# Prompt attention of a two-layer hybrid model: from split fp32r matmuls of one head group to plain fp32 matmuls of two head groups on array halves

## The chip, the core and the metric

The kernel runs on one core of a Trainium2 chip. The metric is the device time of one execution in microseconds (us); the number quoted for a kernel is the median of several executions. TensorE (PE in the profile) multiplies, VectorE (DVE), ScalarE (ACT) and GpSimd (POOL) do elementwise work, SyncE (SP) here only issues DMAs. ScalarE and GpSimd issue DMAs too; each engine takes its instructions in order, DMA issues among them.

## The reference, cut to what matters

Two layers are computed for a prompt of 512 tokens and for a decode batch of 8 sequences with 4 new tokens each. Layer 0 is a gated delta-rule mixer, layer 1 a sparse attention (NSA), each followed by a convolutional feed-forward part. The attention of layer 1 has 16 query heads in 4 groups; a group has one key head and one value head of width 64. Per head, three results are mixed with three learned gates:

```
o_c = attention over compressed blocks of 64 tokens   (raw queries)
o_s = attention over the blocks that o_c selects      (rotated queries)
o_w = attention over a sliding window                 (rotated queries)
out = (g0 * o_c + g1 * o_s + g2 * o_w) @ w_out
```

For the prompt, with 512 tokens and so 8 blocks, `o_s` and `o_w` are both causal attentions over all 512 tokens, with different keys and values. For the decode batch the compressed and the selected keys come from a paged cache in HBM.

## The kernel before, in words

`nsa` runs the attention of layer 1. It has two stages in which several generators ("streams") are merged by `attend`: each stream yields the cost of the piece that it has just emitted, and the stream whose sum of costs is the smallest share of its total goes next. The totals are written by hand: `(22.0, 14.0, 22.0)` for the first stage, `(116.0, 112.0)` for the second. The framework then orders instructions once more with its own model of their times, so an engine's final order can differ from the order in which the code emits them; page loads of the cache are excepted, they stay in the order written. The order of each engine is fixed before the kernel runs.

First stage: `nsa_compress` multiplies cached pages with compression weights (L1523, 8 groups of 32 steps, 64x64 tiles of the array, one accumulator bank of `ps` for each row half). Its page loads (L1467) are issued alternately by SP and POOL, with a page number read from memory ahead of each. Beside it run `cmp_sample` (selection for the decode batch) and `cmp_prompt` (`o_c` of the prompt). `cmp_prompt` reads the eight tiles of raw queries back from HBM through a tile `qx` of two buffers (L1570, SP's queue) and multiplies each (L1571) into one bank.

Second stage: `nsa_sample`, the decode batch, turns cached keys (L1924, copies L1927 and L1929), multiplies scores (L1936), exponentiates and multiplies values (L1995), 16 steps of a sequence and a branch. Beside it `nsa_prompt` works through 32 units (g, n, br): head group g, query head n of it, and branch br (0 for `o_s`, 1 for `o_w`). A unit has three steps, of which one loop pass emits `scores` for unit s, `turn` for unit s-1 and `values` for unit s-2:

- `scores`: every fp32 number is split into a high and a low part of type fp32r. The tile `qs` holds the high part of the query in one half of the 128 rows and the low part in the other; `kh` and `kl` are the parts of the key, in both halves. Each 128 queries take two matmuls (L1780, L1781) of 128x128 weights and 256, 256, 384 or 512 columns. L1783 adds the causal mask and takes the maximum, L1785 exponentiates, L1790 (POOL) scales by gate over sum.
- `turn`: ten transposes (L1805) into three banks, and each bank is split by a cast (L1808, ACT) and a subtraction (L1809, DVE).
- `values`: eight matmuls (L1825) with the high and low part of the values side by side as weights; L1829 and L1830 add the two halves. The result of an even group goes to HBM (`oad`) and is read back when the odd group is done, `o_c` is added (L1837) and the sum goes to `od`.

PSUM has eight banks: two for `po` and `pos`, three for `ps` (nsa_compress and nsa_sample), three for `pp` (nsa_prompt). After the second stage `nsa_out` reads `od` and multiplies with the output weights.

Of the kernel before, what the change touches and what calls it, by code (L numbers as in the profile page):

```python
# [167 lines left out]
class K:  # L168
# [35 lines left out]
    def pool(self, ctx, name, bufs=1, **kw):  # L204
        return ctx.enter_context(self.tc.tile_pool(name=name, bufs=bufs, reuse_waits="tile", **kw))
# [1008 lines left out]
    def nsa(self, nctx, dctx, sctx):  # L1214
# [16 lines left out]
        N['oad'] = [dr.tile([64, 512], F32, name="oad%d" % n) for n in range(4)]  # L1231
        N['kvcd'] = dr.tile([128, 4, 512], F32, name="kvcd")
        with ExitStack() as xctx:
# [44 lines left out]
        for w in self.attend([second(), self.nsa_prompt(kp, ap)], (116.0, 112.0)):  # L1278
            pass
# [269 lines left out]
    def cmp_prompt(self, sp, cP, place):  # L1549
# [182 lines left out]
    def nsa_prompt(self, kp, ap):  # L1732
        nc, N, tc = self.nc, self.N, self.tc
        units = [(g, n, br) for g in range(4) for n in range(4) for br in range(2)]
        KV, QS, PO, EE, PT = {}, {}, {}, {}, {}
        off = (0, 128, 384, 768)

        def keys(g):
            gp, a = divmod(g, 2)
            own, oth = slice(a * 64, a * 64 + 64), slice(64 - a * 64, 128 - a * 64)  # L1740
            for br in range(2):
                kd = kp.tile([128, 512], F32, name="kd", bufs=2)
                for h in (own, oth):
                    nc.scalar.dma_start(kd[h], N['krd'][br][gp][own])
                kh = kp.tile([128, 512], F32R, name="kh%d" % br, bufs=2)
                kl = kp.tile([128, 512], F32R, name="kl%d" % br, bufs=2)
                nc.scalar.copy(kh, kd)
                nc.vector.tensor_tensor(kl, kd, kh.bitcast(F32), op=OP.subtract)
                vs = kp.tile([128, 4, 64], F32, name="vd")
                nc.scalar.dma_start(vs, N['vnd'][br][:, :, g * 64:(g + 1) * 64])  # L1750
                vv = kp.tile([128, 4, 2, 64], F32R, name="v%d" % br, bufs=2)
                nc.scalar.copy(vv[:, :, a, :], vs)
                nc.gpsimd.tensor_tensor(vv[:, :, 1 - a, :], vs, vv[:, :, a, :].bitcast(F32), op=OP.subtract)
                KV[g, br] = kh, kl, vv

        def scores(u):
            g, n, br = u
            gp, a = divmod(g, 2)
            own, oth = slice(a * 64, a * 64 + 64), slice(64 - a * 64, 128 - a * 64)
            if br == 0:  # L1760
                qd = ap.tile([128, 512], F32, name="qd", bufs=1)
                for h in (own, oth):
                    nc.scalar.dma_start(qd[h], N['qrotd'][gp * 4 + n][own])
                qs = ap.tile([128, 512], F32R, name="qs")
                nc.scalar.copy(qs, qd)
                nc.vector.tensor_tensor(qs[oth], qd[oth], qs[oth].bitcast(F32), op=OP.subtract)
                QS[g, n] = qs
            qs = QS[g, n]
            kh, kl, vv = KV[g, br]
            e = ap.tile([128, 1280], F32, name="e")  # L1770
            mn = ap.tile([128, 4], F32, name="mn")
            sm = ap.tile([128, 4], F32, name="sm")
            p2 = None
            for qt in range(4):
                w = 128 * (qt + 1)
                wm = max(w, 256)
                if qt != 1:
                    p2 = self.pp.tile([128, 512], F32, name="pp")
                p = p2[:, 256:512] if qt == 1 else p2[:, :wm]
                nc.tensor.matmul(p, qs[:, qt * 128:(qt + 1) * 128], kh[:, :wm], start=True, stop=False)  # L1780
                nc.tensor.matmul(p, qs[:, qt * 128:(qt + 1) * 128], kl[:, :wm], start=False, stop=True)  # L1781
                ee = e[:, off[qt]:off[qt] + w]
                nc.vector.tensor_tensor_reduce(out=ee, in0=p[:, :w], in1=self.n('tri')[:, 512 - w:], scale=-0.125, scalar=3e38,  # L1783
                                               op0=OP.add, op1=OP.min, accum_out=mn[:, qt:qt + 1])
                nc.scalar.activation(ee, ee, AF.Exp, scale=-1.0, bias=mn[:, qt:qt + 1], accum_out=sm[:, qt:qt + 1])  # L1785
            nc.vector.reciprocal(sm, sm)
            nc.vector.tensor_tensor(sm, sm, N['gtok'][:, :, (g * 4 + n) * 3 + 1 + br], op=OP.mult)  # L1787
            for qt in range(4):
                ee = e[:, off[qt]:off[qt] + 128 * (qt + 1)]
                nc.gpsimd.tensor_scalar(ee, ee, sm[:, qt:qt + 1], 1.0, op0=OP.mult, op1=OP.mult)  # L1790
            EE[u] = e

        poff = (0, 512, 1024, 896)

        def turn(u):
            e = EE.pop(u)
            ph = ap.tile([128, 1280], F32R, name="pth")
            pl = ap.tile([128, 1280], F32R, name="ptl")
            for kts in ((0,), (1, 3), (2,)):
                p = self.pp.tile([128, 512], F32, name="pp")  # L1800
                at = 0
                for kt in kts:
                    for qt in range(kt, 4):
                        c = off[qt] + kt * 128
                        nc.tensor.transpose(p[:, at:at + 128], e[:, c:c + 128], self.ident)  # L1805
                        at += 128
                s = slice(poff[kts[0]], poff[kts[0]] + at)
                nc.scalar.copy(ph[:, s], p[:, :at])  # L1808
                nc.vector.tensor_tensor(pl[:, s], p[:, :at], ph[:, s].bitcast(F32), op=OP.subtract)  # L1809
            PT[u] = ph, pl  # L1810

        def values(u):
            g, n, br = u
            gp, a = divmod(g, 2)
            own, oth = slice(a * 64, a * 64 + 64), slice(64 - a * 64, 128 - a * 64)
            if br == 0:
                PO[g, n] = self.po.tile([128, 512], F32, name="po")
            po = PO[g, n]
            ph, pl = PT.pop(u)
            vv = KV[g, br][2]  # L1820
            for kt in range(4):
                w = 512 - kt * 128
                vw = vv[:, kt].rearrange("p r e -> p (r e)")
                for part in (ph, pl):
                    nc.tensor.matmul(po[:, kt * 128:], vw, part[:, poff[kt]:poff[kt] + w], start=br == 0 and kt == 0 and part is ph,  # L1825
                                     stop=br == 1 and kt == 3 and part is pl)
            if br:
                t = ap.tile([128, 512], F32, name="ot", bufs=1)
                nc.scalar.copy(t[own], po[oth])  # L1829
                nc.vector.tensor_tensor(t[own], po[own], t[own], op=OP.add)  # L1830
                if a == 0:
                    nc.scalar.dma_start(N['oad'][n], t[own])
                else:
                    oc = ap.tile([128, 512], F32, name="oc", bufs=1)
                    nc.scalar.dma_start(t[oth], N['oad'][n])
                    nc.scalar.dma_start(oc, N['ocd'][gp * 4 + n])
                    nc.gpsimd.tensor_tensor(t, t, oc, op=OP.add)  # L1837
                    nc.scalar.dma_start(N['od'][gp * 4 + n], t)

        nu = len(units)  # L1840
        for s in range(nu + 2):
            if s < nu:
                if s == 0:
                    with self.after((self.cmp_done, self.cmp_out)):
                        keys(0)
                if s % 8 == 4 and s < 28:
                    keys(s // 8 + 1)
                with self.after((self.cmp_done, self.cmp_out) if s == 0 else ()):
                    scores(units[s])
                yield 1.2  # L1850
            if 0 <= s - 1 < nu:
                turn(units[s - 1])
                yield 1.1
            if 0 <= s - 2:
                values(units[s - 2])
                yield 1.2
# [270 lines left out]
```

## Time and profile before

| | us |
|---|---|
| median of 3 executions | 2018.57 (2018.2 to 2020.0) |
| the profiled execution | 2023.65 |
| its span, first to last instruction | 2022.0 |
| PE busy in the span | 1913.4 (95%) |
| DVE, ACT, POOL busy | 1138.1, 793.0, 602.6 |

Matmuls are pipelined, so a matmul's duration contains a tail that lies beside the next ones; what a matmul costs the engine is read from the distance of two starts. A plain fp32 matmul appears as two MATMUL instructions in the trace, a transpose and an fp32r matmul as one.

### The profile page before, as it was taken

How to read it: one execution, taken by the hardware profiler on the slowest of the kernel's cores; microseconds unless marked ns; L12 is line 12 of the kernel's file. 1: busy time of each engine (PE TensorE's matmuls, PEld its weight loads, DVE VectorE, ACT ScalarE, POOL GpSimd, SP SyncE). 2: the span in 40 equal slices, each digit the busy share in tenths (PEclk: the TensorE clock that was granted, in tenths of full speed). 3: DMA queues.
4: the chain of work that ended last, by engine and by line, in shares of the span. 5: the costliest groups of instructions: out<-in, count | busy, mean ns of one | idle time of the engine just before them, and what ended most of it. 6: DMA issues, size and time to landing. Idle time of an engine off the chain costs nothing.

```text
span 2022.0 us, 42933 instructions
## 1 busy us (share of the span) xinstructions
PE 1913.4 (95%) x16796; PEld 1756.5 (87%) x16796; DVE 1138.1 (56%) x2215; ACT 793.0 (39%) x1517; POOL 602.6 (30%) x1164
## 2 busy tenths in 40 slices
PE   7999999989999999989989697999997999999997
PEld 7999878879999999989978374676776999999997
DVE  6675586665755655553330024676665476564654
ACT  5543335443433333342210003665754443342335
POOL 2332445112423322301334211233332243241321
PEclk9999989989999999999999787999998999999999
DMA  5222012142222232265578637687576222223221
GB/s 166 87 89 87 11 45 62 42 143 91 80 90 87 84 97 83 76 188 159 170 218 246 190 118 238 193 251 216 171 220 133 91 85 85 84 86 103 77 83 59
DMA packets 225647, 247.07 MB, mean 122 GB/s; under 512 B 29862, under 2 KB 181334, under 8 KB 225188
## 3 DMA queue, kind: packets, MB, share of 16 engines
q1 hardware_dynamic: 196564, 200.09, 32.7%
q10 hardware_dynamic: 19824, 24.72, 4.2%
q0 software_dynamic: 9056, 19.51, 3.3%
q8 instruction: 132, 2.16, 0.4%
q14 instruction: 71, 0.58, 0.1%
HBM read 211.38 MB, written 32.86 MB: 121 GB/s over the span
## 4 chain that ended last, share of the span: by engine, by line
PE 85%; DMA 6%; DVE 4%; ACT 2%; issue 1%; SPq 1%; POOL 0%; ACTq 0%; DVEq 0%; POOLq 0%
PE pdn L424 59%; PE ps L1523 6%; PE po L1825 2%; DMA kv<-in_cache_sel 1%; PE ps L1936 1%; PE pp L1805 1%; PE ps L1924 1%; PE pos L1995 1%; PE ps L847 1%; PE pp L1780 1%; PE ps L857 1%; DMA od<-od 1%; PE pq L1037 1%; PE pp L1781 1%; PE pq L1001 1%
## 5 line engine op out<-in xcount | busy, mean ns | idle before, releaser
L424 PE MATMUL pdn<-hh,whi 128*128 128x272 f32 (+1 forms) x2272 | 477.3, 291 | 3.1 <-ACT hh L323 2.3
L424 PE MATMUL pdn<-hh,wlo 128*128 128x272 f32 (+1 forms) x2272 | 472.1, 289 | 0.0
L424 PE MATMUL pdn<-hl,whi 128*128 128x272 f32 (+1 forms) x2272 | 470.1, 288 | 0.0
L397 ACT CAST whi<-wraw 128x1024 fp32r<-128x1024 f32 (+3 forms) x222 | 214.2, 966 | 454.1 <-PE pdn L424 393.4
L424 PEld LDWEIGHTS pdn<-hh,whi 128*128 128x128 f32 (+1 forms) x2272 | 357.4, 188 | 6.0 <-ACT hh L323 2.7
L424 PEld LDWEIGHTS pdn<-hl,whi 128*128 128x128 f32 (+1 forms) x2272 | 356.7, 188 | 0.7
L424 PEld LDWEIGHTS pdn<-hh,wlo 128*128 128x128 f32 (+1 forms) x2272 | 354.6, 188 | 1.1 <-issue 0.4
L398 DVE TENSOR_TENSOR wlo<-wraw,whi 128x1024 fp32r<-128x1024 f32 (+3 forms) x222 | 250.7, 1130 | 34.7 <-ACT whi L397 27.6
L1133 DVE SCALAR_TENSOR_TENSOR facc<-fext,par,facc 128x592 f32<-128x592 f32 x176 | 146.2, 831 | 19.5 <-ACT facc L1131 16.7
L453 DVE TENSOR_TENSOR xT<-pdn,xT 128x544 f32<-128x544 f32 x80 | 57.7, 724 | 163.9 <-PE pdn L424 163.9
L1126 POOL COPY fext<-fext 128x32 f32<-128x32 f32 x88 | 31.1, 353 | 393.1 <-DVE fext L1123 392.6
L424 PE MATMUL pdn<-gh,whi 128*128 128x272 f32 x704 | 146.3, 289 | 0.2
L424 PE MATMUL pdn<-gh,wlo 128*128 128x272 f32 x704 | 145.2, 288 | 0.3 <-DVE wlo L398 0.3
L424 PE MATMUL pdn<-gl,whi 128*128 128x272 f32 x704 | 144.9, 288 | 0.0
L1523 PE MATMUL ps<-x,wc 64*64 64x128 f32 (+1 forms) x2048 | 135.9, 401 | 7.9 <-DVE cT L1535 5.6
L1523 PEld LDWEIGHTS ps<-x,wc 64*64 64x64 f32 x2048 | 106.6, 155 | 37.1 <-issue 8.4
L1123 DVE TENSOR_TENSOR fext<-pdn,rstd 128x544 f32<-128x544 f32 x88 | 63.6, 725 | 114.0 <-PE pdn L424 113.3
L424 PEld LDWEIGHTS pdn<-gl,whi 128*128 128x128 f32 x704 | 110.0, 188 | 0.3 <-DVE gl L1147 0.2
L424 PEld LDWEIGHTS pdn<-gh,wlo 128*128 128x128 f32 x704 | 109.6, 188 | 0.8 <-DVE wlo L398 0.8
L424 PEld LDWEIGHTS pdn<-gh,whi 128*128 128x128 f32 x704 | 109.4, 188 | 0.8 <-ACT whi L397 0.7
L1790 POOL TENSOR_SCALAR e<-e,sm 128x128 f32<-128x128 f32 (+3 forms) x128 | 66.5, 540 | 110.1 <-DVE sm L1787 38.2
L1131 ACT ACTIVATE facc<-fext,par 128x592 f32<-128x592 f32 x88 | 77.6, 883 | 41.5 <-POOL fext L1126 41.4
(543 smaller groups left out, 3271.1 us busy)
## 6 DMA issues: line engine op xcount, KB each, us to landing
wraw<-in_ffn_w_up SPq DMA_DIRECT2D x40, 1024.0 KB
kv<-in_cache_sel SPq DMA_DIRECT2D x128, 256.0 KB
x<-in_cache_cmp SPq DMA_DIRECT2D x128, 128.0 KB
wraw<-in_gdn_w_in SPq DMA_DIRECT2D x15, 1024.0 KB
wraw<-in_ffn_w_down SPq DMA_DIRECT2D x16, 768.0 KB
x<-in_cache_cmp POOLq DMA_DIRECT2D x96, 128.0 KB, 3.4
wraw<-in_ffn_w_down SPq DMA_DIRECT2D x16, 640.0 KB
kv<-in_state_win SPq DMA_DIRECT2D x16, 512.0 KB
```

The source lines that it names most:

```text
L397: nc.scalar.copy(h, raw)
L398: nc.vector.tensor_tensor(l, raw, h.bitcast(F32), op=OP.subtract)
L424: nc.tensor.matmul(p[:mw, j, :TH], w[:, k, :mw], (x[k] if type(x) is list else x[:, k, :])[:, j * TH:(j + 1) * TH], start=k == 0 and n == ...
L453: self.nc.vector.tensor_tensor(self.two(self.xT[:, m, :]), p, self.two(self.xT[:, m, :]), op=OP.add)
L847: nc.tensor.matmul(p[:, s], B['na'][h][:, s], Y[h][:, s], start=True, stop=True)
L1123: nc.vector.tensor_tensor(self.two(ext[:, 2:2 + T]), p, self.two(rstd), op=OP.mult)
L1126: nc.gpsimd.tensor_copy(se[:, :, 2:6], ext[:, 514:546].rearrange("p (b j) -> p b j", j=4))
L1131: nc.scalar.activation(acc, ext[:, 0:592], AF.Identity, scale=ws[0], bias=self.pcol(f'ffn_b{i}', ft))
L1133: nc.vector.scalar_tensor_tensor(acc, ext[:, j:592 + j], ws[j], acc, op0=OP.mult, op1=OP.add)
L1523: nc.tensor.matmul(p[par][half(f), :n], W[c][half(par), d, :], x[half(par), :n, d], start=k == 0, stop=k == 31)
L1790: nc.gpsimd.tensor_scalar(ee, ee, sm[:, qt:qt + 1], 1.0, op0=OP.mult, op1=OP.mult)
L1825: nc.tensor.matmul(po[:, kt * 128:], vw, part[:, poff[kt]:poff[kt] + w], start=br == 0 and kt == 0 and part is ph, stop=br == 1 and kt == ...
```

## The change

- The prompt's units become 16: (gp, n, br), a pair gp of head groups. Queries, keys and probabilities stay fp32; no part is split.
- `scores`: the two groups of a pair lie in the two halves of the 128 rows. Two matmuls, one for each half of the rows, write to two banks; `pp` has four banks, `ps` two.
- `values`: two matmuls, one for each half of the columns, write to the two halves of one bank; `o_c` is added straight from PSUM. `oad` is gone.
- `turn` copies the transposes once instead of splitting them.
- Keys and values are loaded once, without copies in the other half.
- The raw queries of `cmp_prompt` are loaded from ScalarE's queue.
- The totals and costs for `attend` are rewritten, and `nsa_prompt` yields in smaller pieces.

```
-        N['oad'] = [dr.tile([64, 512], F32, name="oad%d" % n) for n in range(4)]
...
-            self.psum(pctx, 0, 3)
-            self.pp = pool(pctx, "pp", 3, space=PSUM)
+            self.psum(pctx, 0, 2)
+            self.pp = pool(pctx, "pp", 4, space=PSUM)
...
-            for w in self.attend([groups, self.cmp_sample(sp, cT, rest), self.cmp_prompt(sp, cP, x2)], (22.0, 14.0, 22.0)):
+            for w in self.attend([groups, self.cmp_sample(sp, cT, rest), self.cmp_prompt(sp, cP, x2)], (28.0, 14.0, 22.0)):
...
-        for w in self.attend([second(), self.nsa_prompt(kp, ap)], (116.0, 112.0)):
+        for w in self.attend([second(), self.nsa_prompt(kp, ap)], (116.0, 104.0)):
...
-            nc.sync.dma_start(qx, N['qrawd'][j])
+            nc.scalar.dma_start(qx, N['qrawd'][j])
...
+        units = [(gp, n, br) for gp in range(2) for n in range(4) for br in range(2)]
+        half = lambda h: slice(h * 64, h * 64 + 64)
+        def keys(br):
+            for gp in range(2):
+                K[gp, br] = kp.tile([128, 512], F32, name="k%d%d" % (gp, br))
+                nc.scalar.dma_start(K[gp, br], N['krd'][br][gp])
+            V[br] = kp.tile([128, 4, 256], F32, name="v%d" % br)
+            nc.scalar.dma_start(V[br], N['vnd'][br])
...
         def scores(u):
...
+            es = [ap.tile([128, 1280], F32, name="e", bufs=4) for a in range(2)]
...
+            for qts in ((0, 2), (3,), (1,)):
+                p2 = [self.pp.tile([128, 512], F32, name="pp") for a in range(2)]
+                at = 0
+                for qt in qts:
+                    w = 128 * (qt + 1)
+                    ps = [p[:, at:at + w] for p in p2]
+                    at += w
+                    for a in range(2):
+                        nc.tensor.matmul(ps[a], q[half(a), qt * 128:(qt + 1) * 128], k[half(a), :w], start=True, stop=True)
+                    for a in range(2):
...
+                yield 1.72 * at / 1024
...
         def turn(u):
...
+                    if i == 1:
+                        nc.scalar.copy(t[:, s], p[:, :at])
+                    else:
+                        nc.vector.tensor_copy(t[:, s], p[:, :at])
+                PT[u].append(t)
+                yield 1.1
 
         def values(u):
...
             for kt in range(4):
                 w = 512 - kt * 128
+                for a in range(2):
+                    g = 2 * gp + a
+                    nc.tensor.matmul(po[half(a), kt * 128:], V[br][:, kt, g * 64:(g + 1) * 64], ts[a][:, poff[kt]:poff[kt] + w],
+                                     start=br == 0 and kt == 0, stop=br == 1 and kt == 3)
             if br:
+                oc = ap.tile([128, 512], F32, name="oc", bufs=1)
+                nc.scalar.dma_start(oc, N['ocd'][gp * 4 + n])
                 t = ap.tile([128, 512], F32, name="ot", bufs=1)
+                nc.vector.tensor_tensor(t, PO.pop((gp, n)), oc, op=OP.add)
+                nc.scalar.dma_start(N['od'][gp * 4 + n], t)
...
             if 0 <= s - 2:
                 values(units[s - 2])
-                yield 1.2
+                yield 2.15
```

## Rows read from the trace of the kernel before

**Rows 1.** The page: busy shares, 40 slices, and the chain that ended last.
```profile
PE 1913.4 (95%) x16796; PEld 1756.5 (87%) x16796; DVE 1138.1 (56%) x2215; ACT 793.0 (39%) x1517; POOL 602.6 (30%) x1164
...
PE   7999999989999999989989697999997999999997
...
PE 85%; DMA 6%; DVE 4%; ACT 2%; issue 1%; SPq 1%; POOL 0%; ACTq 0%; DVEq 0%; POOLq 0%
```

**Rows 2.** Busy time by stretch: busy us of engines (x instructions), granted clock, DMA share, GB/s.
```profile
1120.00:1165.00 45.00, 26.90 (x239) 14.84 (x234) 4.81 (x14) 1.55 (x4) 11.88 (x23) 0.75 0.59 180
1165.00:1222.00 57.00, 57.00 (x821) 43.53 (x819) 13.45 (x41) 5.96 (x14) 9.68 (x18) 0.91 0.36 111
1222.00:1262.00 40.00, 29.19 (x133) 16.22 (x129) 19.05 (x57) 14.72 (x35) 5.30 (x9) 0.74 0.91 272
1262.00:1540.00 278.00, 263.62 (x3097) 196.32 (x3096) 186.89 (x627) 180.19 (x491) 96.85 (x176) 0.98 0.65 196
```

**Rows 3.** Timeline of 1105 to 1146 us: start, us, engine, line, [idle before].
```profile
1123.42 1.98 PE L1571 MATMUL po<-qx,lb 128*128 128x512 f32 x4
...
1124.46 17.58 SPq L1467 DMA_DIRECT2D x<-in_cache_cmp  x16
...
1131.64 0.42 ACT L1673 ACTIVATE ss<-ss 64x256 f32<-64x256 f32 x1 [19.70 <-DVE ss L1671]
...
1142.15 0.85 SPq L1570 DMA_DIRECT2D qx<-qrawd  x2
...
1145.85 1.22 PE L1571 MATMUL po<-qx,lb 128*128 128x512 f32 x1 [18.10 <-DMA qx<-qrawd]
```

**Rows 4.** Timeline of PE, 1341 to 1345 us: one unit of the prompt.
```profile
1341.27 0.50 PE L1825 MATMUL po<-pth,v 128*128 128x512 f32 x1
...
1344.22 0.28 PE L1781 MATMUL pp<-kl,qs 128*128 128x256 f32 x1
1344.43 0.23 PE L2006 MATMUL ps<-cf,e 64*32 64x64 f32 x1
```

**Rows 5.** Timeline of PE, 1437 to 1441 us: column halves, then transposes.
```profile
1437.48 1.94 PE L1936 MATMUL ps<-kt,qf 128*64 128x512 f32 x8
1439.35 1.31 PE L1805 MATMUL pp<-cf,e 128*128 128x128 f32 x10
1440.50 0.71 PE L1924 MATMUL ps<-cf,kv 128*128 128x128 f32 x5
```

**Rows 6.** Timeline of PE, 287 to 290 us: one row half, one matmul after another.
```profile
287.77 1.93 PE L1037 MATMUL pq<-wg,dkd 64*128 64x512 f32 x4
289.63 0.60 PE L847 MATMUL ps<-Y,na 128*128 128x128 f32 x3
```

**Rows 7.** Timeline of 1207 to 1212 us: row halves and column halves together.
```profile
1207.46 3.69 PE L1523 MATMUL ps<-x,wc 64*64 64x128 f32 x64
...
1211.08 0.50 PE L1634 MATMUL po<-pch,x 128*128 128x512 f32 x1
```

**Rows 8.** Groups of 1240 to 1535 us, shapes apart: busy us, mean ns | idle before.
```profile
L1809 DVE TENSOR_TENSOR ptl<-pp,pth 128x512 fp32r<-128x512 f32 x64 | 43.1, 685 | 14.6 <-ACT pth L1808 13.8
...
L1808 ACT CAST pth<-pp 128x512 fp32r<-128x512 f32 x64 | 36.0, 579 | 16.5 <-PE pp L1805 9.9 <-DMA kv<-in_cache_sel 5.3 <-DVE mn L1958 1.1
L1927 DVE COPY kt<-ps 128x512 f32<-128x512 f32 x38 | 26.1, 687 | 15.4 <-PE ps L1924 15.3
...
L1783 DVE CUSTOM_DVE_ANT_0 e<-pp,cn 128x512 f32<-128x512 f32 x32 | 22.1, 689 | 6.1 <-PE pp L1781 5.7
...
L1929 ACT COPY kt<-ps 128x512 f32<-128x512 f32 x37 | 21.5, 582 | 20.4 <-PE ps L1924 13.6 <-DMA kv<-in_cache_sel 4.7 <-DVE kt L1927 2.0
```

**Rows 9.** Timeline of 1252 to 1254 us: the start of the second stage.
```profile
1252.36 0.62 ACT L1765 CAST qs<-qd 128x512 fp32r<-128x512 f32 x1 [4.00 <-DMA qd<-qrotd]
...
1253.51 3.67 PE L1936 MATMUL ps<-kt,qf 128*64 128x512 f32 x6 [4.02 <-ACT kt L1929]
```

**Rows 10.** Timeline of 1528 to 1562 us: the end of the second stage.
```profile
1538.00 21.52 SPq L1209 DMA_DIRECT2D wraw<-in_nsa_w_out  x16
```

More of the change, by code (lines that the diff above doesn't have):

```diff
@@ L1733, in nsa_prompt @@
         nc, N, tc = self.nc, self.N, self.tc
-        units = [(g, n, br) for g in range(4) for n in range(4) for br in range(2)]
-        KV, QS, PO, EE, PT = {}, {}, {}, {}, {}
+        units = [(gp, n, br) for gp in range(2) for n in range(4) for br in range(2)]
+        K, V, Q, PO, EE, PT = {}, {}, {}, {}, {}, {}
         off = (0, 128, 384, 768)
[L1738 to L1754, printed above, removed]
@@ L1760, in scores @@
             if br == 0:
[L1761 to L1791, printed above, removed]
+                Q[gp, n] = ap.tile([128, 512], F32, name="q")
+                nc.scalar.dma_start(Q[gp, n], N['qrotd'][gp * 4 + n])
+            q, k = Q[gp, n], K[gp, br]
@@ L1793, in nsa_prompt @@
+            for a in range(2):
+                g, sm = 2 * gp + a, sms[a]
+                nc.vector.reciprocal(sm, sm)
+                nc.vector.tensor_tensor(sm, sm, N['gtok'][:, :, (g * 4 + n) * 3 + 1 + br], op=OP.mult)
+                for qt in range(4):
+                    ee = es[a][:, off[qt]:off[qt] + 128 * (qt + 1)]
+                    nc.gpsimd.tensor_scalar(ee, ee, sm[:, qt:qt + 1], 1.0, op0=OP.mult, op1=OP.mult)
+            EE[u] = es
         poff = (0, 512, 1024, 896)
         def turn(u):
-            e = EE.pop(u)
@@ L1797, in turn @@
[L1797 to L1809, printed above, removed]
@@ L1810, in turn @@
-            PT[u] = ph, pl
+            es = EE.pop(u)
+            PT[u] = []
+            for a in range(2):
+                t = ap.tile([128, 1280], F32, name="pt", bufs=4)
+                for i, kts in enumerate(((0,), (1, 3), (2,))):
+                    p = self.pp.tile([128, 512], F32, name="pp")
+                    at = 0
+                    for kt in kts:
+                        for qt in range(kt, 4):
+                            c = off[qt] + kt * 128
+                            nc.tensor.transpose(p[:, at:at + 128], es[a][:, c:c + 128], self.ident)
+                            at += 128
+                    s = slice(poff[kts[0]], poff[kts[0]] + at)
+                    if i == 1:
[4 more added lines that the diff above has]
+                yield 1.1
@@ L1812, in values @@
         def values(u):
-            g, n, br = u
-            gp, a = divmod(g, 2)
-            own, oth = slice(a * 64, a * 64 + 64), slice(64 - a * 64, 128 - a * 64)
+            gp, n, br = u
             if br == 0:
[L1817 to L1820, printed above, removed]
+                PO[gp, n] = self.po.tile([128, 512], F32, name="po")
+            po, ts = PO[gp, n], PT.pop(u)
             for kt in range(4):
@@ L1822, in values @@
                 w = 512 - kt * 128
[L1823 to L1826, printed above, removed]
+                for a in range(2):
+                    g = 2 * gp + a
+                    nc.tensor.matmul(po[half(a), kt * 128:], V[br][:, kt, g * 64:(g + 1) * 64], ts[a][:, poff[kt]:poff[kt] + w],
+                                     start=br == 0 and kt == 0, stop=br == 1 and kt == 3)
@@ L1840, in nsa_prompt @@
+                nc.scalar.dma_start(N['od'][gp * 4 + n], t)
+        with self.after((self.cmp_done, self.cmp_out)):
+            keys(0)
         nu = len(units)
@@ L1842, in nsa_prompt @@
             if s < nu:
-                if s == 0:
[L1844 to L1849, printed above, removed]
-                yield 1.2
+                g = scores(units[s])
+                with self.after((self.cmp_done, self.cmp_out) if s == 0 else ()):
+                    w = next(g)
+                yield w
+                yield from g
+                if s == 0:
+                    keys(1)
             if 0 <= s - 1 < nu:
-                turn(units[s - 1])
-                yield 1.1
+                yield from turn(units[s - 1])
             if 0 <= s - 2:
                 values(units[s - 2])
-                yield 1.2
+                yield 2.15
     def sample_rows(self, kp, rp):
```

20 lines of the change are left out of this document (7 added, 13 removed).

## The prediction, written before the changed kernel ran

> **What bounds the kernel now.** I read the page first. The chain that ended last lies on PE for 85% of the span, PE is busy 95% of it, and the slices show where it is not, the 23rd and 25th above all [rows 1] (1112 to 1163 and 1213 to 1264 us). So a saving counts if it shortens PE's work or its stalls; DVE, ACT and POOL are well below. Then the busy times by stretch [rows 2]. Two stretches are the change's. From 1120 to 1165 us PE works 26.9 of 45 us at a mean granted clock of 0.75. From 1222 us the second stage runs: its first 40 us have 29.2 us of work with the DMA engines at 0.91, and from 1262 to 1540 us PE is busy 263.6 of 278 us. There PE is the bound, and what it idles there (14.4 us) is the most that better cover could return.
>
> Then the timeline of the first stretch [rows 3]. SP starts 16 page loads at 1124.46 and is done with them at about 1142.04; only then, at 1142.15, does it issue the third and fourth load of raw queries. The buffers had been free since the matmuls of 1123.42. PE's next L1571 starts at 1145.85 after 18.10 us of idleness that ends with that DMA. Nothing but the place in SP's queue made it late. Behind it, from 1165 to 1222 us, PE is busy without a gap [rows 2], so the end of the first stage moves with it.
>
> **Part 1: raw queries on ScalarE's queue.** Eight issues move from SP to ScalarE. SP then goes straight to its pages. On ScalarE a waiting issue holds what is behind it: the copies of nsa_compress's sums, for which the accumulator banks wait. ScalarE has room there (1.55 us of work in 45 [rows 2]), but it too takes its instructions in order: its exponential L1673 starts at 1131.64, when it had waited for DVE since 1111 [rows 3]. A load that stands behind L1673 issues at 1132.1 instead of 1142.15, and PE waits 18.1 - 10.1 = 8 us less that stretch of its own work; one that stands ahead of it removes all 18.1. Bounds: -10 and -19 (with the microsecond or so that the first matmul at 1.22 us against half that loses by the clock after the stall). I take -16.5: the third and fourth load need only the two matmuls of 1123.42, and their simulated order will mostly put them before L1673, whose chain is longer. What is late next: the pages of the last group, whose buffer comes free 16 us earlier too, so they move along.
>
> **Part 2: PE's work in the prompt's attention.** One unit of before, 16 fp32r matmuls of scores and values, takes 1344.43 - 1341.27 = 3.16 us from its first start to the start behind its last (the first and the last of the 16) [rows 4]. So two units, which become one, take 6.32 us. (All 512 such matmuls from 1243 to 1538 us sum to 101.9 us from start to next start, 3.18 for a unit.)
>
> After: values are two column halves, the form of L1936, of which eight instructions (four matmuls of 512 columns, in pairs) take 1439.35 - 1437.48 = 1.87 us [rows 5], or 0.913 ns for a column of one matmul. A unit has 2 x (512 + 384 + 256 + 128) = 2560 columns: 2.34 us. Scores have the same 2560 columns on row halves. No row shows that form with both halves alone. Bounds: if both halves stream together, 2.34 us as well; if they take turns, 2560 times the price of L1037, where two such matmuls on one half take 289.63 - 287.77 = 1.86 us for 1024 columns, 1.82 ns each [rows 6]: 4.65 us. The nearest row is L1523, whose tiles use row halves and column halves at once: 64 instructions of 128 columns take at most 1211.08 - 1207.46 = 3.62 us, 57 ns each, while ten transposes of 128 columns after one another take 1440.50 - 1439.35 = 1.15 us, 115 ns each [rows 5, 7]. That is two at a time of four, which column halves alone could explain. I take 2.34 us, because columns and rows enter a tile in the same way there and no pair is seen to queue.
>
> The Trainium skill ("TensorE: Matmul & The Clock Gate", Part 3) says that tiles in different row groups run concurrently, 3.07 times as fast for four. L1523 shows two at a time, so the trace bears out less than the page; by the page the scores cost 2.34 us, by the lower reading of the trace 4.65.
>
> Each piece of work on halves is entered from, and left for, 128x128 work of the other stream. A unit has four such pieces (three of scores, one of values). Bounds: nothing, and a whole pipeline tail at both ends, 1.31 - 1.15 = 0.16 us each as the tail of the transposes [rows 5], 0.32 a piece. I take 0.15, 0.6 us a unit. Sum: 2.34 + 2.34 + 0.6 = 5.28 against 6.32, -1.04 a unit and -16.6 us over 16 units. The transposes stay as many: nothing.
>
> **Part 3: fewer banks for the decode batch.** `ps` goes from three banks to two. A sequence takes 21 banks (14 for the selected branch, 6 for the window, 1 at the end), 168 in all. Each waits for the copy two takes earlier instead of three: L1929 of 582 ns or L1927 of 687 [rows 8]. Between two turns lies a piece of the prompt of about 1 us, which covers such a copy unless ScalarE or VectorE is late. Bounds: nothing, and half of the takes with a whole copy exposed, 84 x 0.64 = 54 us. I take 0.05 us for each, +8.4, since PE idles only 14.4 us of 278 now, with two streams that already collide. `pp` goes to four but scores take them in pairs: VectorE drains the widest pair in 2 x 689 ns [rows 8]. I take +2 for it (bounds 0 and +8). In nsa_compress a group needs both banks at once; only the second of a group waits longer, by one copy, about 0.3 us on five borders: +1.5.
>
> **Part 4: what VectorE, ScalarE and GpSimd lose.** The splits go (96 casts and 96 subtractions become 96 copies on one engine each, those of 512 columns at 579 or 685 ns [rows 8]), and those of keys and queries, and the adding of halves. Some 60 us of ScalarE and 40 of VectorE vanish in the second stage, all beside PE's work: nothing by itself, but it is why part 3's waits stay small. One cast did cost: at 1252.36 ScalarE had waited 4.00 us for a query's DMA, the copy L1929 stood behind it, and PE idled 4.02 us for that copy [rows 9]. Without the cast PE itself waits for the query; I take -3 (bounds -4 and 0). The `oad` round trips and GpSimd's L1837 are beside the decode work. At the end the output weights are requested at 1538.00, when the attention's memory is free [rows 10]; that stays and moves along.
>
> **Sum:** -16.5 - 16.6 + 8.4 + 2 + 1.5 - 3 = -24.2, against the profiled execution's 2023.65: 1999.5. The median of the executions, 2018.57, lies 5.1 below that execution, so the forecast for the median is 1994.4.
>
> **The rivals.**
> - *Row halves take turns* (the other side). Place: L1780's successor; price (4.65 - 2.34) x 16 = 37 us. The sum becomes +12.8, 2031. It decides from 24 us on, that is when a pair takes more than 3.86 us, two thirds of the way from together to in turn. For: no row shows contiguous fp32 on both row halves; L1523 runs two of four at a time. Against: its four instructions would have to be paired by column only.
> - *The stall moves.* The queries queue on ScalarE behind something that waits as long (L1673 or a sum), or the page loads that SP issues earlier make the DMA late. Then part 1 gives nothing: 1994.4 + 16.5 = 2011. For: ScalarE is in order and did wait until 1131.64 [rows 3]. Against: that wait ends 10 us before SP's.
> - *Two banks starve the decode batch*, 0.15 us on each of 168 takes, 25 us: 2011. For: evacuation shares engines with the prompt. Against: part 4's relief.
> - *Every change of array shape costs a whole tail*: 0.32 instead of 0.15 for 64 pieces, +10.9: 2005. The Trainium skill ("TensorEngine Tiling (Array Packing)", Key Properties) says that a change of tiling mode drains TensorE. The ten transposes behind column halves take 115 ns each, too little for a drain ahead of them beyond 0.1 us [rows 5]: the trace agrees in part at most.
>
> **How the numbers follow.** Forecast 0.54 (own range 1983 to 2004), turns 0.09, moved stall 0.13, two banks 0.14, shape 0.10. The changes of 0.2%, 4 us, that this kernel's executions can tell apart lie at 2014.5 and 2022.6. The first, third, fourth and fifth case are faster but for a tenth or so of the moved stall and of the banks, where both come together: faster 0.86, same 0.05, slower 0.09. The range 1974 to 2012 leaves out the turns and a tenth above, and reaches down to where part 1 gives 19, part 2 keeps 0.6 us a unit (no price of a piece, 26 us), part 3 is nothing and part 4 gives 4: 2018.6 - 49 = 1970, of which little is likely.
>
> **What will show it.** Part 1: no idle time of over 3 us ahead of L1571's successor, the first kv load some 16 us earlier than now. Part 2: a pair of 512-column score matmuls starts within a few ns and a unit of scores spans about 2.5 us of PE; with turns, starts 0.43 us apart. Part 3: idle time of PE before the successors of L1924 and L1936 that ends with kt copies, under 10 us more than now. Wrong would be: the second stage as long as now with PE less busy (banks), or longer with PE as busy (turns).

## The result, and the profile after

The changed kernel takes 2037.81 us (median of 5 executions, 2033.19 to 2040.63) against 2020.0 for the kernel before on the same chip (5 executions, 2018.2 to 2024.68): ratio 1.0081, 95% interval 1.0065 to 1.0097. The forecast was 1994.4, range 1974 to 2012. It was wrong, in sign too. The profiled execution of after took 2040.42 us, its span is 2038.7.

The page of after, busy times and PE's 40 slices, as in [rows 1]:

```profile
PE 1939.5 (95%) x16796; PEld 1729.7 (85%) x16796; DVE 1095.6 (54%) x2151; ACT 746.8 (37%) x1405; POOL 585.5 (29%) x1148
...
PE   7999999989999999989989889999986999999997
```

The instruction count of PE is the one of before (16796), and DVE, ACT and POOL lost 42.5, 46.2 and 17.1 us of work. But PE is busy 26.1 us longer, and its weakest slices now lie at the 30th and 31st, at 1478 to 1580 us. The busy times by stretch show where; first the stretches of [rows 2], then the end of the second stage (columns: us, busy us of PE, PEld, DVE, ACT and POOL with instruction counts, granted clock, DMA share, GB/s):

```profile
1120.00:1165.00 45.00, 36.97 (x434) 25.73 (x434) 8.98 (x29) 3.36 (x6) 16.14 (x31) 0.79 0.70 219
1165.00:1222.00 57.00, 51.80 (x727) 42.10 (x723) 13.72 (x41) 8.75 (x19) 5.37 (x10) 0.93 0.54 180
1222.00:1262.00 40.00, 39.83 (x361) 21.45 (x358) 23.54 (x96) 22.18 (x69) 13.93 (x27) 0.93 0.60 199
1262.00:1540.00 278.00, 262.07 (x2545) 149.99 (x2542) 132.03 (x491) 116.84 (x324) 67.77 (x136) 0.95 0.51 166
...
1262.00:1462.00 200.00, 197.98 (x1660) 106.89 (x1661) 110.24 (x410) 97.23 (x281) 61.00 (x121) 1.00 0.44 146
1462.00:1502.00 40.00, 33.09 (x537) 23.52 (x537) 9.78 (x41) 10.06 (x24) 4.00 (x8) 0.79 0.65 203
1502.00:1542.00 40.00, 32.63 (x370) 20.45 (x367) 12.01 (x41) 10.77 (x23) 3.11 (x7) 0.87 0.70 226
```

The first stage did gain: the stretch from 1120 us has 37.0 us of work instead of 26.9, and the last matmul of the compression starts at 1205.3 us instead of 1219.8. The second stage lost more: from that matmul to the first one with the output weights it takes 363.7 us instead of 331.1. From 1262 to 1462 us PE is all but full (198.0 of 200 us), with 0.44 of the DMA engines' time, since it goes through the prompt and not the decode batch and its pages. At 1462 us DVE and ACT fall to a quarter of their time, and the granted clock, 1.00 until then, is 0.79 on average in the next 40 us: the prompt's last matmul started at 1461.2, and the decode batch is alone until 1559.8. In before both end together, at 1537.0 and 1537.8.

To add this up I gave each instant of PE in the second stage to the matmul that started last, so that the pipelined tails count once, and called the rest idle (all us; the kernels below `after` are the experiments; "half clock" is the time at the lower of the two granted clocks, 1.2 instead of 2.4 GHz; "alone" is from the last value matmul of the prompt to the last of the decode batch):

| kernel | ratio to before | scores | values | decode batch | PE idle | half clock | alone |
|---|---|---|---|---|---|---|---|
| before | 1 | 51.9 | 49.9 | 151.0 | 25.4 | 30.7 | 0.9 |
| after | 1.0081 | 63.8 | 56.4 | 162.4 | 26.7 | 47.8 | 98.6 |
| banks33 | 1.0057 | 72.6 | 54.2 | 156.0 | 14.6 | 20.5 | 33.6 |
| twin | 0.9955 | 46.9 | 59.9 | 155.6 | 20.1 | 31.9 | 57.6 |
| twin_v | 0.9897 | 47.9 | 41.8 | 155.9 | 25.5 | 39.3 | 50.4 |
| after_tied | 0.9994 | 53.1 | 56.4 | 154.0 | 26.4 | 20.9 | 9.3 |
| tied | 0.9815 | 46.7 | 41.6 | 143.2 | 15.9 | 10.5 | 2.7 |
| two_banks | 1.0085 | 53.7 | 48.6 | 151.3 | 39.6 | 45.5 | 62.9 |
| two_banks_tied | 1.0068 | 50.5 | 52.0 | 153.0 | 38.5 | 58.3 | 8.6 |

The counts start a few microseconds into the stage. From the last compression matmul on, the idle time is 43.9 us in `two_banks` and 42.5 us in `two_banks_tied`, some 4 us over the table; in the other kernels it is within 0.5 us of it.

After against before: scores +11.9, values +6.5, decode batch +11.4, idle +1.3. The scores and values that were to fall by 16.6 us rose by 18.4.

Why they rose is seen in a few lines. PE in after around 1303 us (start, us, engine, line, operation, tiles, shapes, count; two MATMUL records are one plain fp32 matmul):

```profile
1303.31 1.12 PE L1763 MATMUL pp<-k,q 64*128 64x512 f32 x2
1304.36 0.86 PE L1811 MATMUL po<-pt,v 128*64 128x384 f32 x4
1305.15 1.12 PE L1763 MATMUL pp<-k,q 64*128 64x512 f32 x2
1306.20 0.86 PE L1811 MATMUL po<-pt,v 128*64 128x256 f32 x6
```

One half of a pair of scores (x2) runs alone from 1303.31 to the next start at 1304.36, 1.05 us; its partner runs alone from 1305.15 to 1306.20, again 1.05 us. Between them stands other work. Now the experiment `tied`, in which a pair stands together:

```profile
1299.98 1.13 PE L1764 MATMUL pp<-k,q 64*128 64x512 f32 x4 [0.31 <-DVE pt L1798]
1301.04 0.65 PE L1812 MATMUL po<-pt,v 128*64 128x256 f32 x4
```

Both halves (x4) take 1.06 us. So row halves do stream together, and a half that has no partner beside it costs as much as two. In the order of PE in after, 26 of the 32 score matmuls of 512 columns stand alone and 3 pairs stand together; of the values' matmuls, 28 of 32 with 512 columns and all 32 with 384 stand apart from the partner of their width. The costliest groups by shape show the same without a timeline (line, engine, operation, tiles, shape, count, busy us, mean ns, idle before). After:

```profile
L1763 PE MATMUL pp<-k,q 64*128 64x512 f32 x64 | 32.9, 656 | 0.0
L1811 PE MATMUL po<-pt,v 128*64 128x512 f32 x64 | 32.2, 618 | 0.0
L1811 PE MATMUL po<-pt,v 128*64 128x384 f32 x64 | 27.3, 508 | 0.0
```

And `tied`:

```profile
L1764 PE MATMUL pp<-k,q 64*128 64x512 f32 x64 | 18.0, 640 | 1.9 <-DVE pt L1798 1.9
L1812 PE MATMUL po<-pt,v 128*64 128x512 f32 x64 | 17.3, 618 | 0.0
L1812 PE MATMUL po<-pt,v 128*64 128x384 f32 x64 | 13.6, 504 | 0.0
```

The same count and nearly the same mean duration, at half the busy time: where busy time is far below count times mean, instructions ran beside each other. 64 times 0.64 us is 41 us, which cover 18.0 us of the engine's time when pairs stand, and 42 cover 32.9 when they don't.

The end of the stage, PE's waits in after from 1462 to 1560 us (engine, tile and line, what it waited for: us, times, longest):

```profile
PE ps L1986 <- POOL e L1961: 6.4, 8, 1.0
PE ps L1957 <- DVE mn L1920: 4.7, 7, 1.4
PE ps L1916 <- DVE kt L1907: 2.8, 4, 0.9
PE ps L1968 <- POOL e L1961: 2.0, 7, 0.4
```

These are the decode batch's own steps (scaling, maximum, copies), each a wait of at most 1.4 us, and no work of the prompt is left to fill it. PE idles 19.4 of the 98.6 us, and for 41.0 of them the granted clock is at its lower level.

### The profile page after: what moved, and what is told of

It reads as the page before. It is cut to its first block, busy times and chain, and to the rows that moved or that the text cites. A ratio compares the mean times of both kernels' runs of the same rounds, so it can differ in the third digit from the quotient of the medians.

```text
span 2038.7 us, 42582 instructions
## 1 busy us (share of the span) xinstructions
PE 1939.5 (95%) x16796; PEld 1729.7 (85%) x16796; DVE 1095.6 (54%) x2151; ACT 746.8 (37%) x1405; POOL 585.5 (29%) x1148
## 5 line engine op out<-in xcount | busy, mean ns | idle before, releaser
L1133 DVE SCALAR_TENSOR_TENSOR facc<-fext,par,facc 128x592 f32<-128x592 f32 x176 | 146.2, 832 | 20.5 <-ACT facc L1131 17.6
L1522 PE MATMUL ps<-x,wc 64*64 64x128 f32 (+1 forms) x2048 | 129.9, 401 | 7.8 <-DVE cT L1534 5.9
L1522 PEld LDWEIGHTS ps<-x,wc 64*64 64x64 f32 x2048 | 105.8, 156 | 33.6 <-issue 7.2
L1768 ACT ACTIVATE e<-e,mn 128x128 f32<-128x128 f32 (+3 forms) x128 | 71.0, 556 | 76.8 <-DVE mn L1766 69.2
```

The costliest lines, as they stand in the source:

```text
L1133: nc.vector.scalar_tensor_tensor(acc, ext[:, j:592 + j], ws[j], acc, op0=OP.mult, op1=OP.add)
L1522: nc.tensor.matmul(p[par][half(f), :n], W[c][half(par), d, :], x[half(par), :n, d], start=k == 0, stop=k == 31)
L1768: nc.scalar.activation(ee, ee, AF.Exp, scale=-1.0, bias=mn, accum_out=sms[a][:, qt:qt + 1])
```

## The experiments

Ratios are to the kernel before on the same chip, from 4 to 12 executions of each experiment, but for the last, which ran once; differences between two experiments in us are differences of ratios times 2020.

**The queue alone** (`qx_only`: before, with one line changed).

```
-            nc.sync.dma_start(qx, N['qrawd'][j])
+            nc.scalar.dma_start(qx, N['qrawd'][j])
```

> The kernel before with one edit: the raw queries go through ScalarE's queue. Theory A (the first stage gave what was forecast, the loss of the changed kernel is all in the second stage): the compression ends some 15 us earlier, as it does in the changed kernel (1205.3 against 1219.8 us for the last L1523 matmul), and the whole is 12 to 16 us shorter than before, near 2006. Rival (the stall moves on and the second stage starts no earlier, because its first cache pages or its keys are late anyway): within 4 us of before, near 2020.

Ratio 0.9964 (0.9950 to 0.9977), 7 us: between the two. The last compress matmul starts at 1217.6, 2.2 us earlier. The stall shrank from 18.10 to 13.60 us:

```profile
1123.68 1.98 PE L1571 MATMUL po<-qx,lb 128*128 128x512 f32 x4
1124.85 0.36 SPq L1539 DMA_DIRECT2D cc<-in_c_n  x1
1125.73 16.46 SPq L1467 DMA_DIRECT2D x<-in_cache_cmp  x15
1137.79 1.75 ACTq L1570 DMA_DIRECT2D qx<-qrawd  x2
1141.62 1.22 PE L1571 MATMUL po<-qx,lb 128*128 128x512 f32 x1 [13.60 <-DMA qx<-qrawd]
```

The third load issues at 1137.79, though its buffer is free from 1124.8 and ScalarE has no work from 1111.1 on. It stands ahead of L1673, so not that wait held it, either. What did is the last experiment's question. The time fell by 7 us and the end of the compression by 2.2; where the rest arises stays open.

**A pair's banks as one tile** (`twin`: the changed kernel with two-bank tiles for scores and transposes; the number of banks is the same, and a piece of transposes now covers both groups).

```
-            self.pp = pool(pctx, "pp", 4, space=PSUM)
+            self.pp = pool(pctx, "pp", 2, space=PSUM)
...
-                p2 = [self.pp.tile([128, 512], F32, name="pp") for a in range(2)]
+                p2 = self.pp.tile([128, 2, 512], F32, name="pp")
```

> The changed kernel with the prompt's banks taken two at a time, as one tile of two banks (two such tiles), for scores and for transposes; the arithmetic is the same. Theory A (row halves do stream together, but the two matmuls of a pair stand apart in PE's order because their banks come free one by one, so that most run alone): all pairs stand together; PE's time for scores falls from 63.8 us (start to next start) to 42 to 46, and the whole is 15 to 22 us shorter than the changed kernel, near 2018. Rival B (row halves take turns): scores stay at 60 us or more and the whole within 5 us of the changed kernel. Rival C (the loss is in the two banks of the decode batch and the prompt's running ahead): scores fall, but the whole gains under 8 us.

Ratio 0.9955 (0.9937 to 0.9972), 25 us under the changed kernel. All score pairs but one of 256 columns now stand together, and scores fall from 63.8 to 46.9 us, a little short of A's 42 to 46. Theory A held, with more than its 22 us: the decode batch took 6.8 us less and PE idled 6.6 us less, beside a shorter lonely stretch (57.6 us instead of 98.6). Taking turns, B, is excluded.

**Values in pairs too** (`twin_v`: `twin`, and the second half ordered directly behind the first).

```
-                for a in range(2):
+                first = ()
+                for a in (1, 0):
...
+                    with self.after(first):
+                        first = (nc.tensor.matmul(po[half(a), kt * 128:], ...).ins,)
```

> As twin, and in the values step the matmul of the second head group is issued first and the other's directly behind it, so that the two column halves of a width stand together. Theory A: values fall from 56.4 us of PE to 40 to 44 as well, and the whole is 25 to 36 us shorter than the changed kernel, near 2006. Rival B (halves take turns): no change of either. Rival C (running ahead): under 12 us shorter than the changed kernel, with the decode batch still alone for over 80 us at the end.

Ratio 0.9897 (0.9878 to 0.9916), 37 us under the changed kernel, a microsecond more than A's range; values 41.8 us as A expected. Before that edit the widths of the first half stood ahead of their partners, so that most matmuls met at best one of another width. That the first half ran ahead because its probabilities became ready earlier is likely, but was not tried by itself.

**Three banks each** (`banks33`: the changed kernel with the bank numbers of before).

```
-            self.psum(pctx, 0, 2)
-            self.pp = pool(pctx, "pp", 4, space=PSUM)
+            self.psum(pctx, 0, 3)
+            self.pp = pool(pctx, "pp", 3, space=PSUM)
```

> The changed kernel with three banks for the decode batch and three for the prompt, as before the change. Theory A (split pairs): the pairs stand further apart with a bank less (no pair of 512 columns is together), scores rise to 66 us or more; the decode batch is faster, so the whole is within 8 us of the changed kernel. Rival C (two banks slow the decode batch and let the prompt run ahead, so that the decode batch is alone at the end for 99 us with idle PE and a lower clock): the lonely stretch falls under 50 us and the whole is 15 to 25 us shorter than the changed kernel, near 2017.

Ratio 1.0057 (1.0036 to 1.0077). As A expected: with three single banks no pair of 512 columns stands together at all (32 of 32 alone), scores take 72.6 us, and the shorter lonely end (33.6 us, as C expected) and lower idle time make it only 5 us faster than the changed kernel, not C's 15 to 25. With three banks each the prompt still ends 33.6 us early, so the split of the banks makes 65 of the 98.6 lonely us, not all of them.

**Both streams tied together** (`tied`: `twin_v`, each unit's first score matmul ordered behind a transpose of the decode batch, and the prompt's total for `attend` lowered from 104 to 80; `after_tied`: the same two edits on the changed kernel with its single banks).

```
-        for w in self.attend([second(), self.nsa_prompt(kp, ap)], (116.0, 104.0)):
+        self.mark = {}
+        for w in self.attend([second(), self.nsa_prompt(kp, ap)], (116.0, 80.0)):
...
+                        self.mark[b, br, ch] = nc.tensor.transpose(...).ins
...
-                with self.after((self.cmp_done, self.cmp_out) if s == 0 else ()):
+                tie = [self.mark[k] for k in [((s - 0) // 2, 0, s % 2 * 2)] if k in self.mark]
+                with self.after((self.cmp_done, self.cmp_out) if s == 0 else tie):
```

> The paired version (twin_v) with each prompt unit's first score matmul ordered behind a transpose of the decode batch (L1904's successor), two units to a sequence, so that the order of PE lets both streams end together. Theory A, the lonely tail of the decode batch costs: in twin_v the decode batch is alone for some 50 us (1474 to 1524) with PE idle and its clock down; here alone under 15 us, PE's idle time in the second stage falls from 25.5 to under 18 us, half-clock time from 39 to under 30, time 5 to 12 us under twin_v, near 1995. Rival B, the decode batch is held by its own chain whatever lies beside it: within 4 us of twin_v. Rival C, holding the prompt back makes PE wait in the middle: idle over 30 us, slower than twin_v by over 4.

Ratio 0.9815 (0.9796 to 0.9833): 1983.79 us against 2021.25, 17 us under `twin_v`, and the fastest kernel here. Idle 15.9 us, half clock 10.5, alone 2.7: theory A, with more than its 12 us. The prompt's own work did not change (46.7 and 41.6); the decode batch's fell by 12.7 us of PE, while PE spent 29 us less at the lower clock. "The tie" below means both edits; the order and the total were not tried one by one.

> The changed kernel with the same ordering of the prompt behind the decode batch, but with its single banks, so that pairs stand apart as far as the banks part them. Theory A, split pairs are the main loss and running ahead the smaller one: scores still 55 us or more and values 50 or more of PE's time, the decode batch alone under 20 us instead of 99, time 4 to 14 us under the changed kernel, near 2028, not under before. Rival B, running ahead is the main loss: 22 us or more under the changed kernel, 2015 or less, with scores and values as long as there. Rival C, it does not matter: within 4 us of the changed kernel.

Ratio 0.9994 (0.9980 to 1.0007), 18 us under the changed kernel, equal to before: between A and B. The tie also brought some pairs together (scores 63.8 to 53.1, under A's 55), so not all of it is the lonely end: of PE's time in the stage, 10.7 us came from scores, 8.4 from the decode batch and 0.3 from idle time. Pairing gives 37 us without the tie and 36 with it, the tie 18 without pairing and 17 with it. So pairing is the larger cause. The 18 and the 17 are alike in size but not in kind: with paired banks the tie's gain lies in idle time (9.6 us) and the decode batch (12.7), without them more than half lies in scores. That the two causes simply add is therefore not shown.

**The queue, undone** (`qx_back`: the changed kernel with SP's queue).

```
-            nc.scalar.dma_start(qx, N['qrawd'][j])
+            nc.sync.dma_start(qx, N['qrawd'][j])
```

> The changed kernel with the raw queries issued by SP again. Theory A, the compress stage's 14.5 us (1205.3 against 1219.8) come from the order of engines that two banks and the new totals give, and not from the queue: last compress matmul within 4 us of 1205, time within 4 us of the changed kernel. Rival B, they come from the queue: last compress matmul near 1219, 10 to 16 us slower than the changed kernel. Rival C, both are needed for a part: 4 to 10 us slower.

Ratio 1.0139 (1.0117 to 1.0162), 12 us over the changed kernel. The last compress matmul starts at 1210.3, 5.0 us later: C by the stage. By time it falls into B's 10 to 16 us, while its profiled span is 2.9 us longer only; where the rest arises I did not find out.

**The banks alone** (`two_banks`: before, with two banks of `ps` and four of `pp`), and the same **tied** (`two_banks_tied`, four old units to a sequence, the prompt's total lowered from 112 to 80).

```
-            self.psum(pctx, 0, 3)
-            self.pp = pool(pctx, "pp", 3, space=PSUM)
+            self.psum(pctx, 0, 2)
+            self.pp = pool(pctx, "pp", 4, space=PSUM)
```

> The kernel before with two banks of ps and four of pp, nothing else. It has the old arithmetic. Theory A, the split of the banks by itself sends the prompt ahead and leaves the decode batch alone: prompt's last values matmul 30 us or more ahead of the decode batch's last, PE's idle time in the second stage 8 us or more over 25.4, and the compress stage 10 to 15 us shorter; the time within 8 us of before as the two meet. Rival B, banks cost nothing in the second stage: idle within 4 us of 25.4, so that with a shorter compress stage the time falls by 10 or more. Rival C, the compress stage does not gain by it: last compress matmul within 4 us of 1219.8, and the time 4 us or more longer.

Ratio 1.0085 (1.0067 to 1.0103). The prompt runs ahead (alone 62.9 us), idle rises by 14.2 us, and the compression ends 9.0 us earlier. A's mechanism, but the loss is 17 us where A had the two meet within 8.

> The kernel before with two banks of ps and four of pp, and with each prompt unit's first score matmul ordered behind a transpose of the decode batch, four of the old units to a sequence. The old arithmetic, the new split of the banks, and no running ahead. Theory A, the 17 us that the split of the banks cost (two_banks against before) come from the prompt running ahead: the decode batch alone under 15 us instead of 63, PE's idle time in the second stage back from 39.6 to under 28 us, time 12 us or more under two_banks, and 0 to 14 us under before, as the compress stage ends some 9 us earlier. Rival B, two banks starve the decode batch: idle stays over 33 us with the streams side by side, time within 6 us of two_banks. The new arithmetic with its pairs kept together (tied, ratio 0.9815) then stands 20 us or more below this kernel if the matmuls bring what their starts say.

Ratio 1.0068 (1.0043 to 1.0092). Rival B by its signs: the streams end 8.6 us apart, and idle stays at 38.5 us. From 1262 to 1462 us, with both streams at work, `two_banks` and then `two_banks_tied`:

```profile
1262.00:1462.00 200.00, 185.24 (x2062) 143.70 (x2060) 143.90 (x484) 141.04 (x393) 76.29 (x136) 1.00 0.61 191
```

```profile
1262.00:1462.00 200.00, 181.00 (x1960) 141.00 (x1959) 126.21 (x420) 119.39 (x329) 64.63 (x117) 0.91 0.63 197
```

PE idles 14.8 and 19.0 us, against 8.0 in `tied`, which has the same two banks for the decode batch:

```profile
1262.00:1462.00 200.00, 192.00 (x2348) 115.32 (x2346) 111.94 (x436) 103.42 (x295) 59.13 (x118) 0.99 0.64 207
```

That two banks starve the decode batch does not follow from this. Their price would be waits for the copies of turned keys (`kt`), and in `two_banks_tied` those are not the bulk (1225 to 1500 us; engine, tile and line, what it waited for: us, times, longest):

```profile
PE ps L1938 <- ACT kt L1931: 5.8, 5, 2.9
PE po L1826 <- ACT pth L1809: 4.9, 7, 1.6
PE pp L1781 <- DVE mn L1784: 3.1, 1, 3.1
```

All waits for `kt` in that stretch come to 8.5 us in before with three banks, 14.4 in `two_banks`, 8.1 in `two_banks_tied`, 4.0 in `after_tied` and 0.9 in `tied`. So two banks cost some 6 us of such waits in `two_banks`; the idle time of `two_banks_tied` ends more often with the prompt's own casts, sums and maxima. `after_tied`, with the new arithmetic and the same two banks, still idles 13.3 us from 1262 to 1462 us, so the lighter load of ScalarE and VectorE is not all of `tied`'s advantage, either. Tying the old kernel brought it no gain clear of noise. (The tie moved its first stage too: the last compress matmul is at 1216.2 instead of 1210.8.)

**What the query load waited for** (`pages_pool`: `qx_only` with the compression's page loads on GpSimd's queue only).

```
-        self.page_queues(('sync', 'gpsimd'))
+        self.page_queues(('gpsimd',))
```

> The kernel before with the raw queries on ScalarE's queue and all page loads of the compression on GpSimd's queue instead of SP's and GpSimd's in turn; its time is not the point. In the kernel with the queries alone moved, ScalarE had no work from 1111.1 to 1137.8 us, and the third query load still issued only at 1137.79, 0.53 us after a page load of SP that reports to the same completion semaphore (1137.26). Theory A, the load waited for that page load: with no page loads on SP it issues within 3 us of the end of the second of PE's query matmuls. Rival B, it waited for PE's release of the buffer or for its place on ScalarE: it issues 10 us or more after that matmul here too.

The load issues at 1177.23, while the query matmuls that started at 1176.07 still run:

```profile
1176.07 1.98 PE L1571 MATMUL po<-qx,lb 128*128 128x512 f32 x4
1177.23 4.68 ACTq L1570 DMA_DIRECT2D qx<-qrawd  x3
1180.42 1.12 PE L1571 MATMUL po<-qx,lb 128*128 128x512 f32 x2
```

Theory A. (Slower page loads make that kernel 2096.23 us long, which is not its point.) The trace of `qx_only` shows the way of it. Just ahead of the third load, ScalarE's queue waits for the semaphore that this load is to report to. The last of the 16 landings of an earlier page load of SP on that semaphore came at 1137.71, the wait ended at 1137.75 and the load issued at 1137.79. The expectation above has 1137.26 for that landing; the trace has 1137.71, 0.08 us before the issue. The fourth load does the same on its own semaphore: last landing at 1139.15, issue at 1139.21.

## Why the prediction was wrong

**Part 2 is the step that failed**: "I take 2.34 us, because columns and rows enter a tile in the same way there and no pair is seen to queue." The price of a pair that stands together was near, and the choice between together and in turn was right. With all pairs standing (`tied`) a unit costs 46.7 / 16 = 2.92 us of scores and 41.6 / 16 = 2.60 of values, 5.52 against the 5.28 predicted and 6.36 in before ((51.9 + 49.9) / 16). In after it costs 3.99 and 3.53, 7.51 in all: the term of -16.6 us came out as +18.4. What I took for granted is that the two instructions of a pair follow one another. In L1523 [rows 7], from which I argued, they do: four tiles write to banks that are taken together. Here each half waits for a bank of its own, the banks come free one after another, and the ordering puts other ready work between them. No rival held this: "row halves take turns" has the same price, but as a property of the array, and its sign in the trace ("0.43 us apart") is not what the trace shows; the partner comes 1.84 us later. The prediction could have seen it: the order is fixed by the framework, as the section on the kernel before says, and pairs were priced as if the code's order were the engine's. After takes 63.8 + 56.4 = 120.2 us for what in pairs takes 88.3. The Trainium skill ("TensorE: Matmul & The Clock Gate", Part 3) has tiles in different row groups run concurrently. The traces agree for two: 1.06 us for both halves of 512 columns, 1.05 for one.

**Part 3 priced the wrong thing.** It counted waits for a bank, take by take. What the split of the banks did in after is to give the prompt four banks and so let it run ahead, with the decode batch alone at the end for 98.6 us (33.6 with three banks each), 41.0 of them at half clock. With the pairs kept together, the tie is worth 17 us. Two banks need not mean more waits: `tied`, with two, idles less than before. The rival "two banks starve the decode batch" is borne out by some 6 us of waits for `kt` in `two_banks`, against its 25; for the rest of the old kernel's idle time it stays open. Part 4's relief was put down as nothing by itself. Between `two_banks_tied` and `tied` PE's idle time falls by 22.6 us; 12.1 of them lie between `two_banks_tied` and `after_tied`, which share the tie and single banks, so the relief may be worth up to that. It was not tried alone.

With both put right the change gives more than was forecast: `tied` is 37 us under before, against 24. How that excess divides was not tried.

**Part 1 was right in its sum by luck; its reason is at most a third of it.** The compression ends 14.5 us earlier in after (-16.5 predicted). The queue alone gives 2.2 at the end of the stage and 7 in time, outside the bounds of 10 and 19; two banks and SP's queue give 9.0 in `two_banks` and 9.5 in `qx_back`; the queue adds 5.0 to that. In after the first query matmuls stand at 1093.85 instead of 1123.4 us:

```profile
1093.85 1.98 PE L1570 MATMUL po<-qx,lb 128*128 128x512 f32 x4
1104.41 4.01 ACTq L1569 DMA_DIRECT2D qx<-qrawd  x2
1111.22 1.12 PE L1570 MATMUL po<-qx,lb 128*128 128x512 f32 x2
1116.17 2.08 PE L1570 MATMUL po<-qx,lb 128*128 128x512 f32 x2 [3.83 <-DMA qx<-qrawd]
```

With two banks and SP's queue (`qx_back`) they stand as early, but one wait of 17.49 us remains; on ScalarE's queue it falls apart into waits of 3.83, 1.52 and 4.87 us. Why the matmuls stand earlier with two banks stays open. "The stall moves" named a wait behind L1673 or behind page loads that make the DMA late. It did move, to the page loads, but by way of a completion semaphore: the load on ScalarE's idle queue issued 0.08 us after one of SP's page loads had landed on the semaphore that both report to. So "nothing but the place in SP's queue made it late" was wrong. In before, too, the third load's semaphore took its last page landing at 1136.93, so the queue can have cost at most the 5.2 us from there to 1142.15.

**Part 4's cast** can't be told apart: from 1222 to 1262 us PE is busy 39.8 us instead of 29.2, but the prompt starts 18.5 us earlier there (1225.2 instead of 1243.7). The cast was not tried by itself.

Of the two signs named as wrong, the second came: the stage was longer with PE as busy, which the prediction read as turns. It was split pairs, which look the same in a sum of busy time and different in a timeline.

## What to carry to other kernels

Work that is cheap only in pairs has to be made a pair in the engine's order: one tile for both outputs, or an explicit order behind the first half. Before pricing array halves, ask what releases each half, and look in the trace at whether partners are neighbours.

When a stream gets more buffers, ask who ends last: a stream that runs ahead leaves the other one's small waits bare. Tying the two, with the prompt's total lowered, was worth 17 us here and cost a few lines.

## What the runs showed of the hardware

- A matmul of 64 rows and 512 columns in plain fp32 takes 1.05 us of PE alone and 1.06 us with its partner in the other row half.
- An issue on an engine with nothing else to do can wait for another engine's transfer: 13 us in `qx_only`, between a buffer free at 1124.8 and an issue at 1137.79, 0.08 us after the last landing on the semaphore that the load was to report to; gone when SP had no page loads.
- With the decode batch alone in after, PE's granted clock was at its lower level (1.2 GHz) for 41.0 of 98.6 us, though PE was busy 79.2 of them and no wait was longer than 1.4 us. From 1262 to 1462 us, where PE idled 2.0 us, it was 1.00 (2.4 GHz); in `two_banks_tied`, with both streams at work but PE idle for 19.0 us of the same stretch, it was 0.91 on average.
